# The weights' tiles of a two-block transformer kernel put at fixed places within 512 bytes of SBUF

## The chip, the cores and the metric

The kernel runs on one core of a Trainium2 chip. The metric is device time of one execution in microseconds (us). An execution holds the whole computation: there is one launch, and everything that the host prepares beforehand (transposed or concatenated constants) lies outside the time.

## What is computed

Two stacks of two layers each work one after the other on one activation `x` of 256 tokens by 1024 channels, all in float32:

```python
x = layer_norm(x)
for l in range(2):                                   # first stack
    proj = x @ w_in[l]                               # 1024 x 6816
    na, df, mla = neighbourhood(proj), differential(proj), latent(proj)
    g = sigmoid(gates(proj) + b_gate[l])             # 3 x 1024
    x = layer_norm(a * x + (g0*(na @ wb0) + g1*(df @ wb1) + g2*(mla @ wb2)) @ w_out[l])
    gate, up = split(x @ w_ffn_in[l])                # 1024 x 5632
    x = layer_norm(a * x + (silu(gate) * up) @ w_ffn_out[l])
for l in range(2):                                   # second stack
    q, k, v, u, vv = split(rms_norm(x) @ w_in_2[l])  # 1024 x 1792
    x = x + concat(rms_norm(gqa(q, k, v)), rms_norm(spatial_gating(u, vv))) @ w_o[l]
    h = conv3(rms_norm(x) @ w_up[l])                 # 1024 x 5632
    x = x + (silu(gate(h)) * up(h)) @ w_down[l]
```

With 256 tokens, nearly all of the work is the product of x (or of a hidden activation) with a large weight matrix that is used once.

## The kernel before, in words

**Three products for one.** TensorE multiplies in a rounded float32 format (`float32r`). To keep float32 precision, each operand is split into an upper part (rounded copy) and a lower part (what rounding left), and `mm3` (L247 to L252) issues three matmuls into one PSUM accumulator: upper times upper (L250), upper times lower (L251), lower times upper (L252). In all three the operand named first is the stationary one, which is loaded into the array ahead of its matmul, and the second is the moving one, which is streamed through.

**Units.** A weight matrix comes from HBM in chunks into one of 3 `raw` buffers (`load`, L170, issued by SyncE). A chunk is cut into units of 128 x 1024 elements or less. ScalarE copies the upper part of a unit into a tile of the pool `s4` (`high`, L182 to L184), VectorE subtracts it from `raw` into a second tile of the same pool (`low`, L186 to L188). `pump` (L193) makes units ahead of their use, at most `ahead` of them. The order of all instructions is written out by hand, step by step, with no scheduler.

**Two ways to multiply.** `gemm_a` (L260) takes the activation as the stationary operand, 128 tokens at a time, and streams the weights, up to 512 columns in one matmul; the output has tokens on partitions. The projections that need tokens on partitions, the out-projections and the down-projections of the feed-forward parts use it. `gemm_b` (L322) takes the weights as the stationary operand, 128 columns at a time, and streams the activation, 256 tokens; the output comes transposed. Most of the up-projections of the feed-forward parts, the gates, the branch projections and two of the attention projections use it. One unit of 128 x 1024 in `gemm_b` is 24 matmuls (2 x 4 stationary blocks of 128 columns, three matmuls each), one in `gemm_a` is 12 matmuls of 512 columns (2 column chunks or 2 row blocks, 2 token halves, three each).

**Where things lie.** `x_tok` (the activation), its transpose's upper and lower parts `xh` and `xl`, and constants lie in the pool `const`. The transposed activation x^T is at byte 10,368 (`xh`) and 18,560 (`xl`) of each partition, and each of its blocks of 128 channels takes 1024 bytes, so every block begins 128 bytes past a multiple of 512. The pool `s4` has 30 slots (`S4_BUFS`) of `S4_SLOT` = 1024 + 16 floats, 4160 bytes, from byte 55,936 on. It holds the units' upper and lower parts, and nearly all larger intermediate tiles too: the hidden activations, the gates, the queries and keys, the transposed attention outputs. Slot n begins at 55,936 + 4,160 n, which is 128 + 64 n past a multiple of 512: a tile's place within 512 bytes follows from the slot that happens to be free, and takes each of the eight multiples of 64. In this document the **place** of a tile is its first byte's address modulo 512, and the **distance** of two tiles is the stationary one's place minus the moving one's, modulo 512. Addresses are those of the built program's table. The smaller tiles (`s2` pool, 2048 bytes each) begin at place 0, and the identity matrix that TensorE's transposes stream (`fixed`) at place 288.

Of the kernel before, what the change touches and what calls it, by code (L numbers as in the profile page):

```python
# [10 lines left out]
F32 = mybir.dt.float32  # L11
F32R = mybir.dt.float32r
# [5 lines left out]
P = 128  # L18
D = 1024
# [14 lines left out]

RAW_BUFS = 3
S4_BUFS = 30
S4_SLOT = D + 16
S2_BUFS = 12
AHEAD_ATT, AHEAD_FFN, AHEAD_HOLD, AHEAD_EDGE = 7, 7, 6, 11
TAIL1, HOLD1 = 9, 8  # L40
# [6 lines left out]
class Unit:  # L47


    def __init__(self, raw, off, k0, nk, n):  # L50
        self.raw, self.off, self.k0, self.nk, self.n = raw, off, k0, nk, n
        self.hi = self.lo = None
        self.first = self.last = self.used = False


# [55 lines left out]
class Net:  # L111
# [19 lines left out]
        self.count += 1  # L131
        return f"{s}{self.count}"

    def s4(self, shape, dtype=F32):

        t = self.s4p.tile([P, S4_SLOT], dtype, tag="s4", name=self.nm("s4_"))
        dims = shape[1:]
        t = t[:, :math.prod(dims)]
        if len(dims) == 1:
            return t  # L140
        names = "abcdefg"[:len(dims)]
        return t.rearrange(f"p ({' '.join(names)}) -> p {' '.join(names)}", **dict(zip(names, dims)))
# [12 lines left out]
    def emit(self):  # L155
        order, seen = [], set()
        for s in self.steps:
            for u in s.needs:
                if id(u) not in seen:
                    seen.add(id(u))  # L160
                    order.append(u)
        raws = []
        for u in order:
            if not raws or raws[-1] is not u.raw:
                assert u.raw not in raws
                raws.append(u.raw)
        state = {"raw": 0, "unit": 0, "freed": 0, "used": 0, "credit": 0.0}
        nc = self.nc

        def load():  # L170
            if state["raw"] >= len(raws):
                return
            r = raws[state["raw"]]
            state["raw"] += 1
            r.tile = self.rawp.tile([P, r.nk, r.n], F32, tag="raw", name=self.nm("raw"))
            c = 0
            for c0, w in r.segs:
                src = r.w[r.k0 * P:(r.k0 + r.nk) * P, c0:c0 + w].rearrange("(k p) n -> p k n", p=P)
                nc.sync.dma_start(r.tile[:, :, c:c + w], src)
                c += w  # L180

        def high(u):  # L182
            u.hi = self.s4([P, u.nk, u.n], F32R)
            nc.scalar.copy(u.hi, u.raw.tile[:, u.off:u.off + u.nk, :])  # L184

        def low(u):  # L186
            u.lo = self.s4([P, u.nk, u.n], F32R)
            nc.vector.tensor_tensor(u.lo, u.raw.tile[:, u.off:u.off + u.nk, :], u.hi, op=ALU.subtract)  # L188
            u.raw.left -= 1
            if u.raw.left == 0:  # L190
                load()

        def pump(cost):  # L193


            state["credit"] = min(state["credit"] + RATE * cost, CREDIT)
            while state["unit"] < len(order) and state["unit"] - state["freed"] < self.ahead:
                if state["unit"] - state["used"] >= NEAR:
                    if state["credit"] < 1.0:
                        break  # L200
                state["credit"] = max(state["credit"] - 1.0, 0.0)
                i = state["unit"]
                state["unit"] += 1
                for u in order[i:i + 2]:
                    if u.hi is None:
                        high(u)
                low(order[i])

        def low_next():
            i = state["unit"]  # L210
            state["unit"] += 1
            low(order[i])

        self.high = lambda i: high(order[i])
        self.low_next = low_next
        load()
        self.load_rest()
        load()
        load()
        self.load_tables_first()  # L220
        for s in self.steps:
            assert all(u.lo is not None for u in s.needs), "a unit is needed before it is split"
            s.fn()
            state["freed"] += len(s.frees)
            for u in s.needs:
                if not u.used:
                    u.used = True
                    state["used"] += 1
            pump(s.cost)
            due = [f for n, f in self.waiting if n <= 1]  # L230
            self.waiting = [(n - 1, f) for n, f in self.waiting if n > 1]
            for f in due:
                f()
# [87 lines left out]

    def gemm_b(self, units, act, nft, evac, kind="acc"):  # L322

        units[0].first, units[-1].last = True, True
        st = {}

        def mm(u):
            if u.first:
                st["acc"] = [self.psum(kind) for _ in range(nft // 2)]
            for j in range(u.nk):  # L330
                hi, lo = act(u.k0 + j)
                for f in range(nft):
                    c = (f % 2) * 256
                    self.mm3(st["acc"][f // 2][:, c:c + 256],
                             (u.hi[:, j, f * P:f * P + P], u.lo[:, j, f * P:f * P + P]), (hi, lo),
                             u.first and j == 0 and f % 2 == 0, u.last and j == u.nk - 1, skip=True)
            if u.last:
                evac(st["acc"])

        return [Step(lambda u=u: mm(u), [u], cost=u.nk * u.n * 0.00254) for u in units]  # L340
# [65 lines left out]
    def constants(self):  # L406
        nc, a, cp = self.nc, self.a, self.cp
        self.x_tok = cp.tile([P, 2, D], F32, name="x_tok")
        self.xh = cp.tile([P, KT, 256], F32R, name="xh")
        self.xl = cp.tile([P, KT, 256], F32R, name="xl")  # L410
        cp.tile([P, X_PAD], F32, name="pad")
        self.neghalf = cp.tile([P, 20], F32, name="neghalf")
        nc.vector.memset(self.neghalf, -0.5)
        self.ones = cp.tile([P, 1], F32, name="ones")
        nc.vector.memset(self.ones, 1.0)
        self.fixed = cp.tile([P, a["c_fixed"].shape[1]], F32, name="fixed")
        self.col = cp.tile([P, a["c_vectors"].shape[1]], F32, name="col")
        self.neglam = cp.tile([P, DEPTH], F32, name="neglam")
        for c in range(2):
            cs = slice(c * 512, c * 512 + 512)  # L420
            nc.sync.dma_start(self.x_tok[:, 0, cs], a["x"][0, :P, cs])
        nc.sync.dma_start(self.fixed[:, :P + 2 * KT], a["c_fixed"][:, :P + 2 * KT])
        self.ident = self.fixed[:, :P]
        self.ln_in = [self.fixed[:, P + i * KT:P + (i + 1) * KT] for i in range(2)]
        o = P + 2 * KT

        def table(n):
            nonlocal o
            o += 4 * n
            return self.fixed[:, o - 4 * n:o].rearrange("p (a t n) -> p a t n", a=2, t=2)  # L430

        self.rope_df, self.rope_mla, self.rope_gqa = table(16), table(32), table(64)
        self.mask = self.fixed[:, o:o + 64]
# [956 lines left out]
```

## Time and profile before

| | |
|---|---|
| three runs | 1519.69, 1521.33, 1521.69 us; median 1521.33 |
| the profiled execution's own time | 1521.32 us |
| its span, first to last instruction | 1519.1 us |
| TensorE matmul / VectorE / ScalarE busy | 1487.0 / 991.4 / 820.7 us |
| mean granted TensorE clock | 0.994 of full speed |
| weights and constants read from HBM | 257.86 MB |

The profile is one execution, recorded by the hardware. The span leaves out 2.2 us of the execution's time that lie before its first and after its last instruction. Matmuls overlap in the pipeline, so TensorE counts as busy while one is in flight, and its busy share does not tell how fast matmuls follow one another: that is read from the distance of their start times, which is called the **pace** here.

### The profile page before, as it was taken

To read this page: it belongs to the slowest core of one execution; us is meant where nothing else is said; L and a number is where in the kernel's file an instruction comes from. 1 tells how busy PE (TensorE), PEld (TensorE's weight loads), DVE (VectorE), ACT (ScalarE), POOL (GpSimd) and SP (SyncE) were. 2 spreads that over 40 slices of the span, in tenths; PEclk is the share of its full clock that TensorE was granted. 3 is DMA by queue.
4 is the path that set the end of the run, shared out by engine and by line. 5 is a ranking of instruction groups with operands and counts; after the bars stand their busy time and mean duration, and the time that the engine had idled before them with its cause. 6 is when DMAs were issued, how large, how long until landed. Compare 5 with 4: busy or idle time off the path is not lost.

```text
span 1519.1 us, 23795 instructions
## 1 busy us (share of the span) xinstructions
PE 1487.0 (98%) x9616; PEld 1319.3 (87%) x9616; DVE 991.4 (65%) x1434; ACT 820.7 (54%) x1387; POOL 85.1 (6%) x116
## 2 busy tenths in 40 slices
PE   7899999999999999999999999999999999999999
PEld 5789988899988889998889987777999877789987
DVE  6686654865556676555765455876788657669881
ACT  6564565534442565555454353565777545568660
POOL 0010020000000000011000000300000012000000
PEclk9999999999999999999999999999999999999999
DMA  7635575566563554477566553543565735255560
GB/s 247 235 118 164 171 127 175 167 222 195 185 231 98 201 166 139 150 152 182 184 217 189 200 199 133 184 143 118 162 207 182 265 110 172 92 166 167 197 219 28
DMA packets 179021, 260.44 MB, mean 171 GB/s; under 512 B 23648, under 2 KB 122208, under 8 KB 178912
## 3 DMA queue, kind: packets, MB, share of 16 engines
q1 hardware_dynamic: 178912, 258.93, 53.7%
q8 instruction: 75, 1.23, 0.3%
q14 instruction: 34, 0.28, 0.1%
HBM read 257.86 MB, written 1.05 MB: 170 GB/s over the span
## 4 chain that ended last, share of the span: by engine, by line
PE 50%; DVE 2%; issue 0%; ACT 0%; POOL 0%; ACTq 0%; DVEq 0%; POOLq 0%
PE ps L250 16%; PE ps L252 15%; PE ps L251 15%; PE ps L1111 1%; DVE s L188 1%; PE ps L384 1%; PE ps L400 1%; PE ps L615 0%; PE ps L1160 0%; PE ps L1267 0%; PE ps L1150 0%; DVE x_tok L495 0%; DVE st L483 0%; DVE s L482 0%; POOL st L356 0%
## 5 line engine op out<-in xcount | busy, mean ns | idle before, releaser
L188 DVE TENSOR_TENSOR s<-raw,s 128x1024 fp32r<-128x1024 f32 (+2 forms) x468 | 552.8, 1210 | 175.8 <-ACT s L184 128.8
L184 ACT CAST s<-raw 128x1024 fp32r<-128x1024 f32 (+2 forms) x468 | 465.5, 1039 | 115.2 <-PE ps L251 25.5
L250 PE MATMUL ps<-xh,s 128*128 128x256 f32 x1664 | 473.6, 285 | 1.3 <-DVE s L711 0.6
L251 PE MATMUL ps<-xl,s 128*128 128x256 f32 x1664 | 467.4, 281 | 0.0
L252 PE MATMUL ps<-xh,s 128*128 128x256 f32 x1664 | 467.0, 281 | 0.0
L250 PEld LDWEIGHTS ps<-xh,s 128*128 128x128 f32 x1664 | 314.8, 189 | 9.5 <-issue 6.5
L251 PEld LDWEIGHTS ps<-xl,s 128*128 128x128 f32 x1664 | 314.9, 189 | 0.5
L252 PEld LDWEIGHTS ps<-xh,s 128*128 128x128 f32 x1664 | 314.9, 189 | 0.0
L250 PE MATMUL ps<-s,s 128*128 128x512 f32 (+1 forms) x712 | 261.9, 368 | 0.0
L251 PE MATMUL ps<-s,s 128*128 128x512 f32 (+1 forms) x712 | 257.0, 361 | 0.0
L252 PE MATMUL ps<-s,s 128*128 128x512 f32 (+1 forms) x712 | 257.0, 361 | 0.0
L250 PE MATMUL ps<-s,xh 128*128 128x512 f32 (+3 forms) x448 | 172.8, 386 | 6.6 <-ACT s L664 3.4
L252 PE MATMUL ps<-s,xl 128*128 128x512 f32 (+3 forms) x448 | 170.3, 380 | 2.6 <-DVE xl L345 2.6
L251 PE MATMUL ps<-s,xh 128*128 128x512 f32 (+3 forms) x448 | 169.9, 379 | 0.0
L250 PEld LDWEIGHTS ps<-s,s 128*128 128x128 f32 x712 | 133.8, 188 | 30.5 <-issue 9.5
L252 PEld LDWEIGHTS ps<-s,s 128*128 128x128 f32 x712 | 133.9, 188 | 22.2
L251 PEld LDWEIGHTS ps<-s,s 128*128 128x128 f32 x712 | 134.0, 188 | 20.4
L250 PEld LDWEIGHTS ps<-s,xh 128*128 128x128 f32 x448 | 85.8, 192 | 22.9 <-ACT s L664 3.7
L252 PEld LDWEIGHTS ps<-s,xl 128*128 128x128 f32 x448 | 85.7, 191 | 21.5 <-DVE xl L345 5.7
L251 PEld LDWEIGHTS ps<-s,xh 128*128 128x128 f32 x448 | 85.9, 192 | 15.0 <-DVE s L188 0.5
L355 POOL TENSOR_SCALAR st<-st 128x2 f32<-128x2 f32 (+2 forms) x46 | 19.8, 431 | 989.6 <-DVE st L490 470.1
L394 ACT ACTIVATE s<-ps,st 128x256 f32<-128x256 f32 x96 | 44.6, 472 | 49.1 <-DVE st L391 48.6
(173 smaller groups left out, 1254.6 us busy)
## 6 DMA issues: line engine op xcount, KB each, us to landing
raw<-in_w_in SPq DMA_DIRECT2D x61, 1024.0 KB, 5.1
raw<-in_w_ffn_in SPq DMA_DIRECT2D x88, 512.0 KB, 5.0
raw<-in_w_up SPq DMA_DIRECT2D x88, 512.0 KB, 4.9
raw<-in_w_ffn_out SPq DMA_DIRECT2D x22, 1024.0 KB, 4.9
raw<-in_w_down SPq DMA_DIRECT2D x22, 1024.0 KB, 5.0
raw<-in_w_branch SPq DMA_DIRECT2D x12, 1024.0 KB, 5.1
raw<-in_w_out SPq DMA_DIRECT2D x8, 1024.0 KB, 5.0
raw<-in_w_o SPq DMA_DIRECT2D x8, 1024.0 KB, 5.0
```

The source lines that it names most:

```text
L184: nc.scalar.copy(u.hi, u.raw.tile[:, u.off:u.off + u.nk, :])
L188: nc.vector.tensor_tensor(u.lo, u.raw.tile[:, u.off:u.off + u.nk, :], u.hi, op=ALU.subtract)
L250: mm(out, lh, rh, start=first, stop=False, skip_group_check=skip)
L251: mm(out, lh, rl, start=False, stop=False, skip_group_check=skip)
L252: mm(out, ll, rh, start=False, stop=last, skip_group_check=skip)
L355: self.nc.gpsimd.tensor_scalar(v, src, scale, eps, op0=ALU.mult, op1=ALU.add)
L384: self.nc.tensor.matmul(o[r, :256], vs[:, r] if vs.shape[1] == P else vs, pts[i][:, k * 256:k * 256 + 256], start=k == 0, stop=k == 1)
L394: nc.scalar.activation(p[:, qs], src[:, qs], AF.Exp, bias=nmx[:, q:q + 1], accum_out=sm[:, q:q + 1])
L400: self.nc.tensor.transpose(ps[:, k * 256 + q * P:k * 256 + q * P + P], p[:, q * 256 + k * P:q * 256 + k * P + P], self.ident)
L1111: nc.tensor.matmul(ps[:, q * 256:q * 256 + 256], S["qT"][r, h % 4, q * P:q * P + P], S["kT"][r, :], start=True, stop=True)
```

## The change

The slots of `s4` grow from 4160 to 4608 bytes, which is 9 times 512. All 30 slots then begin at the same place within 512 bytes as x^T: the pool still starts at byte 55,936, place 128. A tile of the pool begins at the start of its slot, with one exception: the parts of a unit that `gemm_b` uses as stationary weights begin 64 bytes (16 floats, upper part) and 192 bytes (48 floats, lower part) into their slots. A unit is marked `stationary` when `gemm_b` lists it. The constant `fixed` moves ahead of an 8-float pad, from place 288 to place 128, and the pools behind `s4` shift with its size: `s2` from place 0 to 128, the small `st` tiles from 0 to 128, the gains `g` and `b` from 0 to 128 as well. `raw` stays where it was.

```diff
-S4_SLOT = D + 16
+S4_SLOT = D + 128
+OFF_HI, OFF_LO = 16, 48
@@ class Unit
         self.hi = self.lo = None
+        self.stationary = False
@@ class Net
-    def s4(self, shape, dtype=F32):
-
+    def s4(self, shape, dtype=F32, off=0):
         t = self.s4p.tile([P, S4_SLOT], dtype, tag="s4", name=self.nm("s4_"))
         dims = shape[1:]
-        t = t[:, :math.prod(dims)]
+        t = t[:, off:off + math.prod(dims)]
@@ emit
         def high(u):
-            u.hi = self.s4([P, u.nk, u.n], F32R)
+            u.hi = self.s4([P, u.nk, u.n], F32R, OFF_HI if u.stationary else 0)
@@
         def low(u):
-            u.lo = self.s4([P, u.nk, u.n], F32R)
+            u.lo = self.s4([P, u.nk, u.n], F32R, OFF_LO if u.stationary else 0)
@@ gemm_b
+        for u in units:
+            u.stationary = True
         units[0].first, units[-1].last = True, True
@@ constants
+        self.fixed = cp.tile([P, a["c_fixed"].shape[1]], F32, name="fixed")
         cp.tile([P, X_PAD], F32, name="pad")
         self.neghalf = cp.tile([P, 20], F32, name="neghalf")
...
-        self.fixed = cp.tile([P, a["c_fixed"].shape[1]], F32, name="fixed")
```

No instruction is added, removed or moved: on each of the five engines the two programs hold the same instructions with the same shapes and tiles in the same order, and each tile gets the same slot number. Only addresses differ. With them, the distances are: 64 and 192 for every matmul of `gemm_b` (upper and lower part stationary, x^T or an activation of the pool moving), and 0 for every matmul of `gemm_a` but those whose unit is 288 columns wide, where a second row block begins 1152 bytes after the first.

## Rows read from the trace of the kernel before

**Rows 1.** The page: span, and busy time of each engine.

```profile
span 1519.1 us, 23795 instructions
...
PE 1487.0 (98%) x9616; PEld 1319.3 (87%) x9616; DVE 991.4 (65%) x1434; ACT 820.7 (54%) x1387; POOL 85.1 (6%) x116
```

**Rows 2.** Groups by line and shape: busy us and mean ns, idle before.

```profile
L188 DVE TENSOR_TENSOR s<-raw,s 128x1024 fp32r<-128x1024 f32 x448 | 534.6, 1221 | 166.2 <-ACT s L184 119.2 <-PE ps L251 23.6 <-PE ps L252 16.3
L250 PE MATMUL ps<-xh,s 128*128 128x256 f32 x1664 | 473.6, 285 | 1.3 <-DVE s L711 0.6 <-ACT s L711 0.5
...
L250 PE MATMUL ps<-s,s 128*128 128x512 f32 x508 | 203.2, 400 | 0.0
...
L250 PE MATMUL ps<-s,xh 128*128 128x512 f32 x352 | 142.4, 404 | 6.6 <-ACT s L664 3.4 <-ACT xh L528 2.9 <-ACT xh L344 0.3
...
L250 PE MATMUL ps<-s,s 128*128 128x256 f32 x204 | 58.6, 288 | 0.0
```

**Rows 3.** What TensorE waited for, longest first: us, times, longest.

```profile
PE ps L520 <- DVE x_tok L513: 6.6, 1, 6.6
```

**Rows 4.** Timeline of TensorE (start, duration): a `gemm_b` unit, distances 64 and 192.

```profile
1420.37 0.28 PE L250 MATMUL ps<-xh,s 128*128 128x256 f32 x1
...
1423.09 0.28 PE L250 MATMUL ps<-xh,s 128*128 128x256 f32 x1
```

**Rows 5.** The same, a `gemm_b` unit with distances 0 and 0.

```profile
364.08 0.28 PE L250 MATMUL ps<-xh,s 128*128 128x256 f32 x1
...
366.96 0.28 PE L250 MATMUL ps<-xh,s 128*128 128x256 f32 x1
```

**Rows 6.** Stretches: us, then busy PE, PEld, DVE, ACT, POOL (count), clock, DMA, GB/s.

```profile
1420.37:1423.09 2.72, 2.72 (x26) 2.72 (x25) 1.90 (x5) 2.65 (x7) 0.00 (x0) 1.00 1.05 340
364.08:366.96 2.88, 2.88 (x26) 2.88 (x25) 0.00 (x0) 0.52 (x2) 0.00 (x0) 1.00 0.53 183
1123.81:1134.69 10.88, 10.88 (x98) 10.88 (x97) 8.93 (x14) 8.09 (x12) 0.00 (x0) 1.00 0.59 186
```

**Rows 7.** Timeline of TensorE: a `gemm_a` unit with distances 0 and 0.

```profile
450.89 0.40 PE L250 MATMUL ps<-s,s 128*128 128x512 f32 x1
...
451.82 0.39 PE L251 MATMUL ps<-s,s 128*128 128x512 f32 x1
...
453.63 0.40 PE L250 MATMUL ps<-s,s 128*128 128x512 f32 x1
```

**Rows 8.** The same, a `gemm_a` unit with distances 0 and 384.

```profile
456.41 0.39 PE L250 MATMUL ps<-s,s 128*128 128x512 f32 x1
...
459.21 0.40 PE L250 MATMUL ps<-s,s 128*128 128x512 f32 x1
```

**Rows 9.** `gemm_b` stretches (first two), `gemm_a` (last two): us, PE busy (count), clock.

```profile
338.51:423.17 84.66, 84.66 (x723) 1.00 0.56 187
...
1087.19:1171.53 84.34, 84.34 (x723) 1.00 0.58 188
...
423.17:482.04 58.87, 58.87 (x257) 1.00 0.57 188
...
1171.53:1230.60 59.06, 59.06 (x257) 1.00 0.63 213
```

**Rows 10.** Timeline of TensorE: a `gemm_b` unit right after transposes.

```profile
1087.39 0.28 PE L251 MATMUL ps<-xl,s 128*128 128x256 f32 x1
...
1088.33 0.28 PE L250 MATMUL ps<-xh,s 128*128 128x256 f32 x1
...
1090.03 0.28 PE L250 MATMUL ps<-xh,s 128*128 128x256 f32 x1
```

**Rows 11.** Chain of waits in order of time: start us, us, what.

```profile
757.69 0.87 PE ps L615 x8
...
942.90 4.54 DVE s L188 x4
```

**Rows 12.** Stretch around the first stack's last layer norm, columns as in rows 6.

```profile
895.00:990.00 95.00, 88.43 (x390) 71.03 (x389) 61.58 (x74) 42.93 (x56) 15.57 (x16) 1.00 0.51 171
```

## Prediction

> **What bounds the kernel now.** I read the page first: TensorE has a matmul in flight for 1487.0 us of the span of 1519.1 us, VectorE is busy for 991.4 and ScalarE for 820.7 [rows 1]. The reader is to see that one engine carries the time. The waits say the same: the longest total that TensorE waited for one releaser is 6.6 us, once, at the start [rows 3]. So what counts is how fast TensorE's matmuls follow one another, and in the views of groups this can't be seen: their means (285 ns for 256 columns, [rows 2]) contain the overlap.
>
> So I went to the timeline and divided the time between two starts by the number of matmuls. Two units of `gemm_b`, with the same 24 matmuls of 256 columns, differ. The one at 1420.37 us takes 1423.09 - 1420.37 = 2.72 us, 113.3 ns each [rows 4]; the one at 364.08 us takes 2.88 us, 120.0 ns each [rows 5]. Neither waited, and the granted clock is 1.00 in both, the 2.4 GHz level [rows 6]. By the table of addresses, the first has its upper part in slot 1 (byte 60,096, place 192) and its lower part in slot 11 (byte 101,696, place 320), distances 64 and 192 from x^T. The second has them in slots 16 and 8 (bytes 122,496 and 89,216), both at place 128, distances 0 and 0. What else runs beside them doesn't explain it, since it points the other way: beside the fast unit VectorE works for 1.90 us, ScalarE for 2.65 and the DMA engines are fully busy; beside the slow one VectorE does nothing, ScalarE 0.52 us [rows 6].
>
> Units of `gemm_a` differ as well, and here distance 0 is good. The unit at 450.89 us has both parts and its stationary activation at place 192 (slots 9, 25 and 1), distances 0. It begins slowly, then does the eight matmuls from 451.82 to 453.63 in 1.81 us, 226.3 ns each [rows 7]. The unit at 456.41 us, with distances 0 and 384 (slots 28 and 6 against 4), needs 2.80 us for 12, 233.3 ns each [rows 8].
>
> What the mix of places costs is read from long stretches of one kind. 30 units of `gemm_b`, 720 matmuls, take 84.66 us, 117.6 ns each; another 30 take 84.34, 117.1 [rows 9]: I use 117.5. 255 matmuls of `gemm_a` take 58.87 us, 230.9 each, and 59.06, 231.6 [rows 9]: I use 231.1. My reading is that the pace follows the distance of the two SBUF streams that TensorE reads, the moving operand of one matmul and the stationary one of the next; that it is the distance modulo 512, whichever slots are involved, rests on a few units and is the step most open to doubt.
>
> **The change part by part.** No instruction moves, so every term is a pace.
>
> *`gemm_b` in the feed-forward parts.* Four times 9 groups of 4 units of 24 matmuls are 3456 matmuls. All get distances 64 and 192, so all should run like [rows 4]: 117.5 - 113.3 = 4.2 ns each, 14.5 us. After something else on TensorE the pace settles first: in a unit after transposes, with distances 320 and 192, the eight matmuls from 1087.39 to 1088.33 us take 0.94 us, still 117.5 each, and the fifteen after them, to 1090.03, 1.70 us, 113.3 [rows 10]. Such an interruption therefore forgoes 8 x 4.2 = 34 ns. There are some three in each of these parts, 0.4 us. **Gain 14.1 us.**
>
> *`gemm_b` in attention.* 1664 triples of matmuls stream x^T [rows 2]; of the 204 with both operands from the pool, 192 belong to `gemm_b` and 12 to `gemm_a`'s 256-column remainder. So 1856 triples, of which 1152 are the ones above, and 704, or 2112 matmuls in 88 units, stand in attention. 2112 x 4.2 = 8.9 us; these units stand between attention steps, and if each is interrupted once, 88 x 34 ns = 3.0 us of it is lost. **Gain 5.9 us.**
>
> *`gemm_a`, 512 columns.* 508 + 352 triples [rows 2], 2580 matmuls, all with distance 0 afterwards. The settled pace I take as 226.6, by [rows 7] with the slow start left out: 231.1 - 226.6 = 4.5 ns, 11.6 us. The start of that unit cost 0.93 us for four matmuls, 24 ns over the settled pace; some 60 pieces of this work give 1.4 us. About 160 of these matmuls end at a wait or run at the 1.2 GHz level and gain nothing, 0.7 us. **Gain 9.5 us.** Bounds: all of the 11.6, or a loss, if the settled state is that of [rows 8], of (233.3 - 231.1) x 2580 = 5.7 us.
>
> *Narrower `gemm_a` units* (256, 288, 384 columns) are few. The 44 triples of 256 columns get distance 0, at which `gemm_b` runs at 120.0 [rows 5]: 132 x 2.5 ns = 0.3 us lost at most. For 96 matmuls each of 288 and 384 columns no row stands at the new distances; between the extremes of the 256-column rows, 113.3 and 120.0 around 117.5, that is under 4% of some 30 us in all, and I take 0 within 1 us either way.
>
> *Transposes and attention's unrounded matmuls.* The identity matrix goes from place 288 to 128, so each transpose gets a distance that no row shows. Eight of them take 0.87 us now, 109 ns each [rows 11]. The program has 568; scaled from the 256-column extremes, which are -4% and +2% of their mean, the bounds are 2.5 us gained and 1.3 us lost. I take 0.
>
> *VectorE, ScalarE, DMA.* Their operands move too, but the copy and the subtraction that make a unit have nothing in the sum: they are hidden behind matmuls. A unit costs VectorE 1221 ns [rows 2]. Four units at 113.3 ns in a row, from 1123.81 to 1134.69 us, in the second stack's feed-forward part, where VectorE has most to do beside its splits, leave VectorE 8.93 us busy of 10.88, ScalarE 8.09 [rows 6]. The cover holds at the pace that I forecast.
>
> *What is given back.* Around the first stack's last layer norm TensorE is busy for 88.43 us of 95 [rows 12], and the chain runs through VectorE there, for instance through four splits that queue behind the norm [rows 11]. A TensorE that is 2% faster reaches these waits sooner and waits longer: at most 95 x 2% = 1.9 us in this stretch. The other norms have shorter waits; I take 1.5 us in all.
>
> Sum: 14.1 + 5.9 + 9.5 - 1.5 = 28.0 us. The profiled execution took 1521.32 us, its span and 2.2 us around it, and lies at the median of the runs, 1521.33. **1521.3 - 28.0 = 1493.3, say 1493 us.** Bounds of this case: with no settling and nothing given back 14.5 + 8.9 + 11.6 = 35.0, 1486; with attention's units never settling, half of `gemm_a`'s gain and the full loss at the norm 14.1 + 4.7 - 1.9 = 16.9, 1504.
>
> **The rivals.** *The `gemm_a` part goes the wrong way.* One unit alone shows distance 0 throughout [rows 7], it was slow at first, and for 256 columns distance 0 is the slow place. At the pace of [rows 8] the sum is 14.1 + 5.9 - 5.7 - 1.5 = 12.8, 1508 us. For it speaks the single unit, against it that this unit settled and stayed.
>
> *The faster matmuls run into their suppliers.* If splits or weight loads can't keep up, half of the gain becomes waits on VectorE: 1507 us. Against it stand the four fast units in a row [rows 6]; a unit needs 1221 ns on VectorE and 2.72 us on TensorE.
>
> *Addresses don't matter.* The pace would then come from something that varies along with the slots, and nothing changes: 1521 us. The rows against it are the two units with like work and clock, where the busier neighbourhood goes with the faster one [rows 4 to 6]. The Trainium skill speaks for this rival: its page "TensorE: Matmul & The Clock Gate", Part 2, says that TensorE has two independent SBUF read ports, so that loading the next weights takes no read bandwidth from the running matmul, and "SBUF — State Buffer", Who interferes with whom, that "PE and ACT never wait on anyone". By that rule the change gives 0 and by the rows 28 us; the trace does not agree with it for this format, as 113.3 and 120.0 ns stand side by side.
>
> *Slower than before: crowding.* Now the 30 slots spread over eight places. If it is not the distance that counts, but how many of the tiles in use share a place, then putting all on one place makes the worst pairing the rule: `gemm_b` at the 120.0 of [rows 5], 5568 x 2.5 ns = 13.9 us, and `gemm_a` at the 233.3 of [rows 8], 5.7 us: 1541 us. It decides as soon as the 64 and 192 bytes do not take `gemm_b` out of the crowd. For it: the unit of [rows 5] has everything on one place. Against it: so has the one of [rows 7], which settles to the fastest pace.
>
> **How the numbers follow.** Forecast 0.78, `gemm_a` the wrong way 0.10, suppliers 0.05, no effect 0.04, crowding 0.03. The range is the forecast's own, 1486 to 1504, reaching down 1 us for transposes and up to the two cases at 1507 and 1508: 1485 to 1508. A measurement of this kernel can tell about 0.2%, 3 us, from no change. Faster by more: 0.93; within: 0.04; slower: 0.03.
>
> **What would show it.** The timeline of the changed kernel should have `gemm_b` units of 2.72 us one after the other (30 in 81.6 us where 84.66 stood), `gemm_a` stretches of 255 matmuls in 57.8 us where 58.87 stood, transposes still at 109 ns, splits still at 1221 ns, and TensorE's waits about 1 to 2 us longer around the layer norms. I am wrong if units still differ among each other, if `gemm_a` stretches don't get shorter, or if waits on VectorE or on weight loads grow by 5 us or more.

## The result, and the profile after

The changed kernel takes **1497.2 us** (median of four runs, 1496.05 to 1497.94) against 1520.5 for the kernel before, measured beside it: a ratio of 0.9847, interval 0.983 to 0.9864. That is 23 us less. The forecast was 1493 us, its range 1485 to 1508.

The page of the changed kernel (span, then busy time and share of each engine):

```profile
span 1493.8 us, 23795 instructions
...
PE 1458.4 (98%) x9616; PEld 1298.9 (87%) x9616; DVE 990.4 (66%) x1434; ACT 820.5 (55%) x1387; POOL 85.6 (6%) x116
```

The span fell by 1519.1 - 1493.8 = 25.3 us. The numbers of instructions are those of before, VectorE and ScalarE are busy for as long as before [rows 1]; TensorE alone does the same work in less time. The profiled execution took 1496.05 us, 2.2 more than its span, as before.

The windows view of the changed kernel over the stretches of [rows 9] in their order, then the units of [rows 5, 8], then the stretch of [rows 12] (columns: window, us, busy time and count of PE, PEld, DVE, ACT, POOL, granted clock, DMA share, GB/s; lines L250 to L252 are now L254 to L256):

```profile
333.03:414.75 81.72, 81.72 (x723) 81.72 (x722) 44.36 (x46) 36.90 (x46) 0.00 (x0) 1.00 0.58 194
1071.35:1153.05 81.70, 81.70 (x723) 81.70 (x722) 73.51 (x113) 62.85 (x95) 0.00 (x0) 1.00 0.59 193
414.75:472.58 57.83, 57.83 (x258) 47.87 (x256) 31.46 (x31) 23.09 (x24) 1.23 (x2) 1.00 0.55 191
1153.05:1210.88 57.83, 57.83 (x258) 47.87 (x256) 34.32 (x38) 27.86 (x35) 0.74 (x2) 1.00 0.62 220
357.63:360.35 2.72, 2.72 (x26) 2.72 (x25) 0.00 (x0) 0.48 (x1) 0.00 (x0) 1.00 0.66 221
447.42:450.14 2.72, 2.72 (x14) 2.25 (x12) 2.36 (x2) 1.08 (x2) 0.00 (x0) 1.00 0.96 352
881.04:975.47 94.43, 87.19 (x389) 71.16 (x388) 61.75 (x75) 43.48 (x56) 15.57 (x16) 1.00 0.50 174
```

The reader is to see that 30 units of `gemm_b` take 81.7 us twice, where 84.66 and 84.34 stood, and 255 matmuls of `gemm_a` 57.83 us twice, where 58.87 and 59.06 stood. Before, two stretches of the same work differed; now they agree to 0.02 us. The unit that took 2.88 us takes 2.72, and so does the `gemm_a` unit that took 2.80.

A pace over the whole program is the mean distance between two starts, over all places where a matmul follows another without a stall (ns; 4852, 592 and 2429 of them after). The last column is the difference times that number:

| | before | after | difference | by count, us |
|---|---|---|---|---|
| `gemm_b` on x^T, 256 columns | 117.49 | 113.66 | 3.83 | 18.6 |
| both operands from the pool, 256 columns | 118.14 | 113.96 | 4.18 | 2.5 |
| `gemm_a`, 512 columns | 231.23 | 227.4 | 3.83 | 9.3 |

These gains make 30.4 us, of which 25.3 arrived in the span: **5.1 us were given back**. Where, the list of TensorE's waits tells (us in total, times, longest). First the changed kernel, of whose 14 rows these are the ones that moved most:

```profile
PE ps L1166 <- ACT st L1091: 5.6, 2, 2.9
PE ps L254 <- ACT s L670: 4.2, 1, 4.2
PE ps L406 <- ACT s L808: 3.4, 2, 1.9
PE ps L254 <- ACT xh L534: 2.2, 1, 2.2
PE ps L621 <- DVE x_tok L501: 0.8, 2, 0.4
```

and the kernel before, whose lines of this code have numbers 6 (in `mm3` 4) lower:

```profile
PE ps L1160 <- ACT st L1085: 4.8, 2, 2.5
PE ps L250 <- ACT s L664: 3.4, 1, 3.4
PE ps L400 <- ACT s L802: 2.5, 3, 1.5
PE ps L250 <- ACT xh L528: 2.9, 1, 2.9
```

All 14 rows make 30.9 us after and 27.7 before: 3.2 us more of waiting. It grew by 0.8 or 0.9 us at each of four places, three of them in attention (L670, L808, L1091) and one behind a norm (L501), and shrank by 0.7 at the first norm (L534). The rest is the clock. The stretches at a granted clock of 0.50, the 1.2 GHz level, make 17 us before and 20.4 after; if a us at half the clock loses half a us, 1.7 more is lost. By this estimate 3.2 + 1.7 = 4.9 of the 5.1 are found. The longest of these stretches after, which has no counterpart before (another, near 238 us, is 3.4 us shorter than before):

```profile
691.30:698.10 6.80, 6.80 (x27) 5.64 (x26) 2.37 (x5) 3.31 (x8) 1.28 (x1) 0.50 0.76 265
```

What TensorE did before the clock fell there, on its timeline (start, duration, and in brackets the idle time before with its releaser):

```profile
688.84 0.28 PE L256 MATMUL ps<-xh,s 128*128 128x256 f32 x1
690.68 1.12 PE L406 MATMUL ps<-fixed,s 128*128 128x128 f32 x4 [1.56 <-ACT s L808]
...
694.33 0.41 PE L256 MATMUL ps<-xh,s 128*128 128x256 f32 x1
...
694.97 0.41 PE L256 MATMUL ps<-xh,s 128*128 128x256 f32 x1
```

It waited for an attention probability that ScalarE had to scale (L808): 690.68 - 688.84 = 1.84 us from start to start, 1.56 of them idle. Three matmuls later on take 0.64 us, 213 ns each, where the mean at the 2.4 GHz level is 113.66. The kernel before waits at this place too, for less:

```profile
702.36 0.95 PE L400 MATMUL ps<-fixed,s 128*128 128x128 f32 x4 [0.70 <-ACT s L802]
```

Its cause is on ScalarE and SyncE. ScalarE's rows are in program order, and the scaling stands behind a cast whose weights were late (the changed kernel's ScalarE timeline, then its SyncE queue, with the time that issuing took):

```profile
688.18 1.05 ACT L188 CAST s<-raw 128x1024 fp32r<-128x1024 f32 x1 [4.98 <-DMA raw<-in_w_branch]
```

```profile
666.12 11.82 SPq L828 DMA_DIRECT2D s<-in_na_rpb  x8
678.35 0.38 SPq L183 DMA_DIRECT2D raw<-in_w_branch  x1
```

Eight small loads of the attention bias hold SyncE's queue for 11.82 us, and the weights are issued behind them. By the records of the eight, issuing takes 9.2 of this (0.6 to 1.35 us for seven of them, 3.34 for one); the rest is waiting, in front of the last load above all, which the list of SyncE's waits puts down to a load of weights still on its way:

```profile
SPq L828 <- DMA raw<-in_w_in: 5.2, 2, 3.0
```

The kernel before has the same pair with 12.49 us for the eight: the queue's time hardly shrinks with TensorE's. Of the four waits that grew, this is the only one that was followed to its cause.

### The profile page after: what moved, and what is told of

The parts are those of the page before. It is cut to its first block, busy times and chain, and to the rows that moved or that the text cites. A ratio compares the mean times of both kernels' runs of the same rounds, so it can differ in the third digit from the quotient of the medians.

```text
span 1493.8 us, 23795 instructions
## 1 busy us (share of the span) xinstructions
PE 1458.4 (98%) x9616; PEld 1298.9 (87%) x9616; DVE 990.4 (66%) x1434; ACT 820.5 (55%) x1387; POOL 85.6 (6%) x116
## 4 chain that ended last, share of the span: by engine, by line
PE 81%; DVE 7%; DMA 5%; ACT 4%; issue 2%; SPq 1%; POOL 1%; DVEq 0%; ACTq 0%; POOLq 0%
PE ps L254 24%; PE ps L256 24%; PE ps L255 24%; DVE s L192 3%; DMA raw<-in_w_in 2%; PE ps L406 2%; DMA s<-in_na_rpb 1%; PE ps L390 1%; DMA raw<-in_w_branch 1%; PE ps L1117 1%; PE ps L818 1%; ACT s L188 1%; SPq L828 1%; ACT s L400 1%; PE ps L621 1%
## 5 line engine op out<-in xcount | busy, mean ns | idle before, releaser
L192 DVE TENSOR_TENSOR s<-raw,s 128x1024 fp32r<-128x1024 f32 (+2 forms) x468 | 552.9, 1209 | 166.6 <-ACT s L188 118.7
L188 ACT CAST s<-raw 128x1024 fp32r<-128x1024 f32 (+2 forms) x468 | 465.9, 1039 | 106.7 <-PE ps L255 26.1
L254 PE MATMUL ps<-xh,s 128*128 128x256 f32 x1664 | 468.0, 281 | 1.4 <-DVE s L717 0.9
L256 PE MATMUL ps<-xh,s 128*128 128x256 f32 x1664 | 461.5, 277 | 0.0
L255 PE MATMUL ps<-xl,s 128*128 128x256 f32 x1664 | 461.5, 277 | 0.0
L254 PEld LDWEIGHTS ps<-xh,s 128*128 128x128 f32 x1664 | 314.1, 189 | 9.6 <-issue 6.5
L256 PEld LDWEIGHTS ps<-xh,s 128*128 128x128 f32 x1664 | 314.1, 189 | 0.0
L254 PE MATMUL ps<-s,s 128*128 128x512 f32 (+1 forms) x712 | 259.2, 364 | 0.0
L255 PE MATMUL ps<-s,s 128*128 128x512 f32 (+1 forms) x712 | 254.5, 357 | 0.0
L256 PE MATMUL ps<-s,s 128*128 128x512 f32 (+1 forms) x712 | 254.5, 357 | 0.0
L254 PE MATMUL ps<-s,xh 128*128 128x512 f32 (+3 forms) x448 | 170.9, 382 | 6.7 <-ACT s L670 4.2
L256 PE MATMUL ps<-s,xl 128*128 128x512 f32 (+3 forms) x448 | 168.7, 377 | 2.8 <-DVE xl L351 2.8
L255 PE MATMUL ps<-s,xh 128*128 128x512 f32 (+3 forms) x448 | 167.7, 374 | 0.0
L254 PEld LDWEIGHTS ps<-s,s 128*128 128x128 f32 x712 | 133.7, 188 | 28.7 <-issue 9.5
L256 PEld LDWEIGHTS ps<-s,s 128*128 128x128 f32 x712 | 133.7, 188 | 20.3
L255 PEld LDWEIGHTS ps<-s,s 128*128 128x128 f32 x712 | 133.8, 188 | 18.5
L254 PEld LDWEIGHTS ps<-s,xh 128*128 128x128 f32 x448 | 85.3, 190 | 22.0 <-ACT s L670 4.5
L256 PEld LDWEIGHTS ps<-s,xl 128*128 128x128 f32 x448 | 85.0, 190 | 20.8 <-DVE xl L351 6.1
```

Of the source, the lines that this page charges most:

```text
L254: mm(out, lh, rh, start=first, stop=False, skip_group_check=skip)
L255: mm(out, lh, rl, start=False, stop=False, skip_group_check=skip)
L256: mm(out, ll, rh, start=False, stop=last, skip_group_check=skip)
```

## The experiments

All are edits of the changed kernel. A ratio is to the kernel before; the median of a run has its range behind it.

### Which of the two formats gives what

**Only `gemm_b` at its new distances.** The weights that `gemm_a` streams are spread over all eight places again:

```diff
+        for i, u in enumerate(order):
+            u.place = i
-            ... OFF_HI if u.stationary else 0)
+            ... OFF_HI if u.stationary else 16 * (u.place % 8))
-            ... OFF_LO if u.stationary else 0)
+            ... OFF_LO if u.stationary else 16 * ((u.place // 8 + u.place) % 8))
```

> The changed kernel with one part undone: gemm_a's weight tiles (the moving ones) take the eight multiples of 64 bytes in turn, upper and lower part independently; gemm_b's stay at 64 and 192. Distance theory: gemm_b keeps its 113.7 ns, gemm_a goes back from 227.4 to about 231.1 ns a matmul, 2580 x 3.7 = 9.5 us, so about 1506.5 us. Crowding theory (what counts is how many tiles share a place): spreading tiles can't hurt, 1497 us or less. If all of the gain were gemm_b's: 1497 us.

Measured: 1505.5 us (1504.15 to 1506.84), ratio 0.9899 (0.9871 to 0.9928). The two stretches, `gemm_b` and `gemm_a`:

```profile
336.98:418.70 81.72, 81.72 (x724) 81.72 (x722) 44.38 (x46) 36.90 (x46) 0.00 (x0) 1.00 0.59 194
418.70:477.62 58.92, 58.92 (x258) 47.88 (x256) 31.58 (x32) 23.02 (x24) 1.23 (x2) 1.00 0.54 187
```

**Only `gemm_a` at its new distances.** The mirror image: the weights of `gemm_b` get the eight places, those of `gemm_a` stay at 0.

> The other part undone: gemm_b's weight tiles (the stationary ones) take the eight multiples of 64 bytes in turn, upper and lower part independently; gemm_a's stay at distance 0. Distance theory: gemm_b goes back from 113.7 to about 117.5 ns, 5568 x 3.8 = 21 us, so about 1518 us, with gemm_a at 227.4. Crowding theory: 1497 us or less.

Measured: 1515.9 us (1513.06 to 1519.04), ratio 0.9958 (0.9945 to 0.9972):

```profile
338.53:423.35 84.82, 84.82 (x724) 84.82 (x723) 44.43 (x46) 36.92 (x47) 0.00 (x0) 1.00 0.56 187
423.35:481.15 57.80, 57.80 (x257) 47.86 (x256) 31.45 (x31) 23.07 (x24) 1.23 (x2) 1.00 0.56 191
```

Each stretch goes back to the time of [rows 9] where its weights are mixed and stays at the new one where they aren't. As shares, 1.0% from `gemm_b` and 0.4% from `gemm_a` come to about the 1.5% of both together. The forecast's two terms stood at 20.0 and 9.5 us; in time, less than that arrives from either alone.

### Is it the place, or the distance?

**All at distance 0.** `gemm_b`'s parts lose their offsets.

```diff
-OFF_HI, OFF_LO = 16, 48
+OFF_HI, OFF_LO = 0, 0
```

> Offsets 0 and 0 instead of 64 and 192: every large tile at the place of x^T. Distance theory: every gemm_b unit runs like the one with distances 0 and 0 in the profile of before, 120.0 ns, 5568 x 6.3 = 35 us more than the changed kernel, about 1532 us, slower than the kernel before; gemm_a stays at 227.4. Crowding theory: slower too, and gemm_a's pace suffers no less than gemm_b's. If only the alikeness of the slots counts: 1497 us.

Measured: 1524.6 us, ratio 1.0033 (1.0015 to 1.0051), slower than the kernel before.

```profile
338.11:424.57 86.46, 86.46 (x723) 86.46 (x722) 44.47 (x46) 36.87 (x47) 0.00 (x0) 1.00 0.55 183
424.57:482.40 57.83, 57.83 (x257) 47.87 (x256) 31.47 (x31) 23.05 (x24) 1.23 (x2) 1.00 0.56 191
```

720 matmuls in 86.46 us are 120.1 ns each: the unit of [rows 5] held for the whole program. The pace came as expected and the median 7 us lower than expected. Part of that is spread: the profiled execution took 1527.82 us, 3.2 above the median. Its waits sum to 31.0 us, no less than the changed kernel's 30.9, so a slower TensorE does not wait less here. 17.1 us run at 1.2 GHz where 20.4 stood, no more of a difference than between two profiles of the changed kernel itself (further down).

**x^T 64 bytes further on, the weights left where they are.** A pad of 64 bytes moves `xh` and `xl` together. A second one behind them makes the shift 512 bytes in all, so that everything behind keeps its place.

```diff
+        cp.tile([P, 16], F32, name="pad_x")
...
+        cp.tile([P, 112], F32, name="pad_y")
```

> x^T alone moves by 64 bytes, all weights and pool tiles keep the places of the changed kernel. The distances of the x-streaming gemm_b matmuls become 0 and 128, those of the x-stationary gemm_a matmuls 64. Distance theory: 4992 matmuls of gemm_b go from 113.7 to about 119.0 ns (units with 0 and 128 in the profile of before), 26 us; 1056 matmuls of gemm_a from 227.4 to about 232.9 (units with 64 and 64 there), 6 us; about 1529 us, while the 576 gemm_b matmuls that stream pool tiles stay at 114. Theory of places (the weights' own addresses count, whatever x^T does) and crowding theory: 1497 us.

Measured: 1523.1 us (1517.61 to 1528.73), ratio 1.0022 (0.9998 to 1.0046). The windows are, in this order: `gemm_b` on x^T (distances 0 and 128), `gemm_b` on pool tiles (64 and 192, as in the changed kernel), `gemm_a` with x^T stationary (64):

```profile
335.37:421.20 85.83, 85.83 (x723) 85.83 (x722) 44.47 (x46) 36.93 (x47) 0.00 (x0) 1.00 0.55 185
260.00:270.78 10.78, 10.78 (x97) 10.78 (x96) 7.29 (x9) 6.65 (x10) 0.00 (x0) 1.00 0.59 190
481.99:491.56 9.57, 9.57 (x43) 7.71 (x42) 8.71 (x12) 3.95 (x6) 1.23 (x2) 1.00 0.05 6
```

No weight tile has moved, and whatever meets x^T is slow: 119.2 ns, and 9.57 us for 41 matmuls of 512 columns, 233.4 each. What meets a pool tile keeps 113.5 (95 in 10.78 us). This is the run that decides between the distance and any theory of the weights' own places: 64 bytes on the other operand take the whole gain.

**x^T moved, and `gemm_b`'s weights moved after it.** The pads stay, and the offsets become 128 and 256 bytes, so that distances to x^T are 64 and 192 again and those to pool tiles 128 and 256.

```diff
-OFF_HI, OFF_LO = 16, 48
+OFF_HI, OFF_LO = 32, 64
```

> x^T moved by 64 bytes as in the run before, and the stationary weights moved by 64 bytes with it. Distance theory: the 4992 x-streaming gemm_b matmuls are back at 64 and 192 and at 113.7 ns; the 576 that stream pool tiles get 128 and 256, about 118.5 to 119 ns (3 us more); the 1056 x-stationary gemm_a matmuls stay at distance 64, 233.4 ns (6 us more); about 1506 us by the changed kernel's own waits. Theory of places: weights at places 256 and 384 are as bad as any mix, 117.5 ns, 1525 us or more.

The same three windows:

```profile
332.92:414.61 81.69, 81.69 (x723) 81.69 (x722) 44.40 (x46) 36.93 (x46) 0.00 (x0) 1.00 0.58 194
258.25:269.49 11.24, 11.24 (x98) 11.24 (x96) 7.72 (x10) 7.12 (x11) 0.00 (x0) 1.00 0.59 189
475.37:484.94 9.57, 9.57 (x42) 7.71 (x41) 8.72 (x12) 3.95 (x6) 1.22 (x2) 1.00 0.04 7
```

`gemm_b` on x^T is back at 113.5 ns, and now the pool's is the slow one, 118.3: each class follows its own distance. The time did not come as expected: 1498.0 us (1495.32 to 1500.69), ratio 0.9855 (0.9816 to 0.9895), as fast as the changed kernel within the spread of its two runs, though its paces cost 576 x 4.4 ns + 1056 x 6 ns = 8.9 us more. In the profiled execution, the faster of the two, the step from start to start ahead of L406 is 0.67 us where 1.84 stood:

```profile
691.34 0.95 PE L406 MATMUL ps<-fixed,s 128*128 128x128 f32 x4 [0.39 <-ACT s L810]
```

The late cast begins at 688.84 us there, 0.66 us later than in the changed kernel, but TensorE reaches the group of L406 before it 1.80 us later (686.25 against 684.45), so it waits less for the same late weights. All waits sum to 28.4 us where 30.9 stood, and 6.8 us run at 1.2 GHz where 20.4 stood, which saves some 6.8 by the estimate above. In this execution less waiting and less of the slow clock made up for what the slower paces cost.

### Which distances are good

**64 for both parts, 32 and 160, and 384 for `gemm_a`.** Three runs that change one number each.

```diff
-OFF_HI, OFF_LO = 16, 48
+OFF_HI, OFF_LO = 16, 16
```

> Offsets 64 and 64: the lower part no longer 128 bytes away from the upper part, both distances odd multiples of 64. If an odd multiple of 64 is all that gemm_b wants: 113.7 ns and 1497 us. By the few units of before with 64 and 64 (115.6 ns on average, some at 113.3 and some at 117.7): the pace settles in one of two states, 115 to 118 ns, 1505 to 1520 us.

```diff
-OFF_HI, OFF_LO = 16, 48
+OFF_HI, OFF_LO = 8, 40
```

> Offsets 32 and 160 bytes instead of 64 and 192: distances that are no multiple of 64, which no row of before shows for these matmuls. If the two streams meet on units of 64 bytes, half a unit is between a good and a bad distance: gemm_b between 114 and 120 ns, 1500 to 1530 us. If what matters is only that the distance is no multiple of 128: 113.7 ns, 1497 us.

```diff
-            u.lo = self.s4(..., OFF_LO if u.stationary else 0)
+            u.lo = self.s4(..., OFF_LO if u.stationary else 32)
```

> The changed kernel with the lower part of gemm_a's moving weights 128 bytes further on: distances 0 (upper) and 384 (lower) everywhere. Distance theory: every gemm_a unit runs like the one at 456.41 us of before, 233.3 ns instead of 227.4, 2580 x 5.9 = 15 us more, about 1512 us, gemm_b unchanged at 113.7. If only the upper part's distance counts, or only that tiles are alike modulo 128: 1497 us.

Measured: 1509.2 us (1508.1 to 1510.24), 0.9914 (0.9891 to 0.9937), with 64 twice; 1520.3 (1515.83 to 1525.61), 0.9995 (0.9974 to 1.0016), with 32 and 160; 1501.5 (1500.67 to 1502.41), 0.9864 (0.9841 to 0.9886), with 384. With 64 twice, the `gemm_b` stretches of the first and of the second stack:

```profile
335.73:417.43 81.70, 81.70 (x724) 81.70 (x722) 44.39 (x46) 36.91 (x46) 0.00 (x0) 1.00 0.58 194
1078.53:1163.41 84.88, 84.88 (x723) 84.88 (x722) 73.60 (x112) 62.83 (x95) 0.00 (x0) 1.00 0.57 187
```

The two run the same instructions at the same distances, 64 for every one of their weight loads, and one holds 113.5 ns from end to end, the other 117.9. So a distance of 64 can be fast, and does not have to be; 64 and 192 in turn were fast in every such stretch seen. The other two stretches of this run take the time of their own stack, 81.70 and 84.88 us, so it is not chance from stretch to stretch. Beside the slow ones VectorE and ScalarE are busier (73.60 and 62.83 us against 44.39 and 36.91); whether that sets the pace, no run tells. At 64 and 192 the same busier neighbours leave it at 81.70 us. With 32 and 160, 720 matmuls take 85.27 us, 118.4 each:

```profile
338.14:423.41 85.27, 85.27 (x723) 85.27 (x722) 44.47 (x46) 36.86 (x47) 0.00 (x0) 1.00 0.56 186
```

With 384, `gemm_a` takes

```profile
415.83:474.76 58.93, 58.93 (x257) 47.88 (x256) 31.61 (x32) 23.07 (x24) 1.23 (x2) 1.00 0.55 187
```

231.1 ns each, no better than the mix and not as bad as the 233.3 of [rows 8]: one unit stood for that distance there, and a long stretch of it averages less.

### What is given back, and whether it can be had

**The changed kernel once more,** to see what of its waits and clock recurs.

> The changed kernel unedited, profiled a second time, to see what its given-back microseconds are. Theory of waits: TensorE reaches the same few waits sooner, so the wait at about 689 us (ScalarE behind a weight load) and the stretches at the 1.2 GHz level after waits (20.5 us in the first profile, 17.1 before the change) recur at the same places, within 0.3% of 1497 us. Theory of chance: they fall elsewhere or are missing, and the time of each execution follows their length, 1.7 us per 3.4 us.

Measured: 1496.0 us (1495.89 to 1498.66), ratio 0.9846 (0.9823 to 0.987), the same paces. The wait ahead of L406 near 689 us recurs (2.32 us from start to start where 1.84 stood) and so does a window at 1.2 GHz behind it, of 3.4 us this time; the one at 237 us is gone, one at 945 is new. The sum at 1.2 GHz is 17.1 us instead of 20.4, all waits make 31.6 us instead of 30.9, and the span is the same to 0.1 us. So the split between waits and clock is not fixed, and the estimate that adds them up is good to about 1 us.

**The bias loads four heads ahead instead of three.** If TensorE waits because these loads come late, they should start earlier.

```diff
-            if h + 3 < 8:
-                na_bias(h + 3)
+            if h + 4 < 8:
+                na_bias(h + 4)
...
-        fill.append(Step(lambda: [na_bias(h) for h in range(3)]))
+        fill.append(Step(lambda: [na_bias(h) for h in range(4)]))
```

> The changed kernel with the neighbourhood attention's bias tiles loaded four heads ahead instead of three. Theory of waits: the wait at about 689 us (1.8 us) and the 6.8 us at 1.2 GHz after it come from SyncE's queue, where a branch weight's load stands behind bias loads; loaded earlier, both shrink, 2 to 5 us less, 1492 to 1495 us. Rival: the bias loads only move to another place of the same queue and the same weight load is late: 1497 us.

Measured: 1506.8 us (1503.43 to 1514.01), ratio 0.9915 (0.9888 to 0.9942): 10 us slower than the changed kernel at unchanged paces. SyncE's queue, ScalarE and TensorE:

```profile
645.64 17.98 SPq L828 DMA_DIRECT2D s<-in_na_rpb  x20
...
674.95 11.20 SPq L828 DMA_DIRECT2D s<-in_na_rpb  x8
686.24 1.10 SPq L183 DMA_DIRECT2D raw<-in_w_branch  x2
```

```profile
698.45 1.04 ACT L188 CAST s<-raw 128x1024 fp32r<-128x1024 f32 x1 [8.63 <-DMA raw<-in_w_branch]
```

```profile
700.95 1.30 PE L406 MATMUL ps<-fixed,s 128*128 128x128 f32 x4 [6.59 <-ACT s L808]
```

Twenty bias loads now keep the queue for 18 us, the branch weights are issued 8 us later than in the changed kernel, and TensorE waits 6.59 us instead of 1.56. The sign was the other one, and the mechanism is seen all the better: not the bias is late, the weights behind it are.

**The bias loads off SyncE's queue, and two heads ahead.** The first issues them from GpSimd, the second starts them later.

```diff
-                    nc.sync.dma_start(b[...
+                    nc.gpsimd.dma_start(b[...
```

> The changed kernel with the bias tiles of the neighbourhood attention loaded from GpSimd's queue instead of SyncE's. In the changed kernel's trace eight of these loads occupy SyncE for 11.8 us from 666.12 us on, the branch weight's load stands behind them, ScalarE waits 5.0 us for it and TensorE 1.8, after which it runs 6.8 us at 1.2 GHz. Theory of waits: without them on SyncE the weights come on time, both neighbourhood stretches (around 233 and 690 us) lose their waits and the slow clock after them, 3 to 8 us less, 1488 to 1494 us. Rival: GpSimd issues them later or its own additions wait for them, and the scores wait instead: 1497 us or more.

```diff
-                na_bias(h + 3)
+                na_bias(h + 2)
...
-        fill.append(Step(lambda: [na_bias(h) for h in range(3)]))
+        fill.append(Step(lambda: [na_bias(h) for h in range(2)]))
```

> The bias tiles two heads ahead instead of three, the opposite of the run with four, which was 10 us slower. Theory of the queue: fewer bias loads stand ahead of the weights' loads, the waits at 233 and 690 us shrink, 1490 to 1496 us. Rival: the bias now comes late for GpSimd's addition (it waits for these loads 204 us in all already), and the scores wait instead: 1500 us or more.

Measured: 1509.0 us (1506.78 to 1515.73), 0.9922 (0.9896 to 0.9948), from GpSimd; 1501.9 (1500.38 to 1503.44), 0.9866 (0.9842 to 0.9891), two ahead. Neither gives anything back. GpSimd's timeline in the first:

```profile
678.89 1.30 POOL L831 TENSOR_TENSOR s<-s,fixed 128x512 f32<-128x512 f32 x1 [7.08 <-DMA s<-in_na_rpb]
680.14 2.44 POOL L828 DMA_DIRECT2D s<-in_na_rpb  x4
689.06 1.28 POOL L831 TENSOR_TENSOR s<-s,fixed 128x512 f32<-128x512 f32 x1 [6.49 <-DMA s<-in_na_rpb]
```

GpSimd also adds the mask to each bias (L831) and waits for one head's load before it issues the next head's. The two additions shown are 10.2 us apart, and TensorE's waits behind L808 sum to 18.5 us instead of 3.4. In the second the bias itself is late, for VectorE, and TensorE's waits behind L808 sum to 9.9 us:

```profile
672.81 0.69 DVE L842 TENSOR_TENSOR s<-ps,s 128x512 f32<-128x512 f32 x1 [5.38 <-POOL s L831]
```

So three heads ahead stands between two kinds of lateness, and no run tried beat the changed kernel. That SyncE's queue holds up the branch weights is shown; that the 5 us could be had by taking the bias out of it is not, since the run for it made a new wait.

## Why the prediction was right, and where it was off

*TensorE carries the time, and its pace is the term.* Right: same instructions, same busy time elsewhere, and 30.4 us of pace. The rival that suppliers would not keep up is out: TensorE's weight loads waited 2.0 us in all for casts and splits of weights (L188, L192), and 1.6 before.

*The pace follows the distance modulo 512.* This was called the step most open to doubt, and it holds in what it was used for. Moving x^T alone spoils it, moving the weights after it restores it, and the class that meets the pool goes the other way. It does not hold as a law: at 64 throughout, two stretches of equal distances ran at 113.5 and 117.9 ns. Nor do the runs tell 512 from 256: no two of the pairs that were tried differ by 256 alone, and the unit of [rows 10], with 320 and 192, settles at the 113.3 ns of 64 and 192, as a step of 256 would have it too. That the streams meet in reading SBUF is the forecast's reading; no run shows what in the chip makes the pace.

*`gemm_b`, 14.1 + 5.9 = 20.0 us.* 21.1 measured. Two sizes made up for one another: 4.2 ns a matmul was taken and 3.8 to 4.2 came, and the settling in attention cost less than the 3 us put down for it.

*`gemm_a`, 9.5 us.* 9.3 measured, at 226.8 ns in long stretches as [rows 7] had it, so the single unit was a fair witness. The rival that this part goes the wrong way is out, and so is crowding: with everything on one place `gemm_b` is slow, at the 120 ns that crowding gave it, and `gemm_a` as fast as ever, where crowding makes both slow.

*Narrower `gemm_a` units, 0 within 1 us.* Right: their paces went from 118.5 to 119.3 ns (256 columns), from 132.6 to 132.4 (288) and from 174.3 to 173.9 (384), under 0.1 us for each of them.

*Transposes and splits unchanged.* Right. The changed kernel's chain of waits has eight transposes in 0.87 us as in [rows 11], and its groups by shape have the splits at 1221 ns as in [rows 2]:

```profile
473.43 0.87 PE ps L621 x8
```

```profile
L192 DVE TENSOR_TENSOR s<-raw,s 128x1024 fp32r<-128x1024 f32 x448 | 534.6, 1221 | 156.4 <-ACT s L188 108.5 <-PE ps L255 24.9 <-PE ps L256 16.7
```

*Given back, 1.5 us.* **This is the term that was mis-sized: it measured 5.1 us**, 3.6 more. Less the 0.9 us that the paces gave beyond the forecast, this makes 2.7 of the 3.9 us between forecast and result. The other 1.2 are spread: the profiled execution of the changed kernel lies 1.15 us below the median of its runs, that of the kernel before lay at it. The step looked for the loss at the layer norms. There it was about right: the stretch of [rows 12] has 94.43 - 87.19 = 7.2 us without a matmul where 95 - 88.43 = 6.6 stood. It left out attention, where three waits grew by 0.8 to 0.9 us each, one of them behind a late load of weights that stands in SyncE's queue behind bias loads. And it priced a wait at its length alone, while a stretch at 1.2 GHz may follow it: behind the 1.84 us at 689 us came 6.8 us of it, some 3.4 us lost by the estimate above. The range was wide enough for this.

*Addresses don't matter.* Out, by eight runs that change addresses alone and take from 1498 to 1525 us. The same 720 matmuls take 86.46 us in the run with everything at distance 0 and 81.72 in the changed kernel. The Trainium skill's "TensorE: Matmul & The Clock Gate", Part 2, has two independent read ports, by which loading weights takes nothing from the running matmul; by that rule alone the two would take the same time, and the trace does not agree.

## What to carry to other kernels

Where matmuls and weight loads of the rounded float32 format follow one another without waits, divide start distances by their number for single units and hold the paces against the addresses of both operands. Going from a mix at 117.5 and 231.2 ns to 113.7 and 227.4 was worth 1.5% of this kernel, for some padding, and the worst distances tried made it 0.3% slower than the mix. Fix the distance of the stationary from the moving operand, not the place of either, and measure each pair over long stretches. And when the bounding engine gets faster, price the queues that do not, since the waits behind them and the slower clock after them took about a sixth of this gain.

## What the runs showed of the hardware that was not expected

- The slow pace adds the same time at both widths, though not at the same distance: 120.1 - 113.5 = 6.6 ns on 256 columns (everything at 0) and 233.4 - 226.8 = 6.6 ns on 512 (x^T moved, at 64). So here it is an amount for each matmul with its weight load, not for each column.
- At equal distances (64 for every load) the pace has two values, 113.5 ns in the first stack and 117.9 in the second, and holds one of them through 720 matmuls. What chooses is open.
- Waits and the granted clock can hide a change of pace: with x^T moved and followed, 8.9 us of slower paces left the span of the profiled execution at 1493.1 us, against 1493.8 in the changed kernel.
- A bias load of 64 KB, in rows of 256 bytes, held SyncE's queue for 0.6 to 3.9 us (median 0.80 of 64 in the changed kernel), and most loads of 1024 KB of weights for 0.37. So bytes do not price a load for the queue here; long ones occur among the weights too, 3.60 us for one of `w_out` at 686.01 us.
